# Rows of three expert pairs fetched from DRAM and transposed in place of one-hot products

## The chip, the cores and the metric

The kernel runs on one core of a Trainium2 chip, and the metric is the device time of one execution in microseconds (us). About 0.5% (5.5 us) is what a timing of this kernel can tell from no change.

## What is computed

A two-layer trunk on 512 tokens of width 1024. Layer 0 mixes with attention and a state-space scan, layer 1 with a chunked mLSTM; behind each mixer stands a layer norm, a mixture of experts with 16 experts of hidden width 256, of which two are chosen for each token, and another layer norm. The change concerns only how the experts get their tokens:

```python
combine = jnp.einsum('tk,tke->te', weights, jax.nn.one_hot(expert_id, N_EXPERTS))
hid = jax.nn.silu(jnp.einsum('td,edf->tef', t, w_gate)) * jnp.einsum('td,edf->tef', t, w_up)
hid = hid * combine[:, :, None]
out = jnp.einsum('tef,efd->td', hid, w_down)
```

## The kernel before

Nearly every matrix product runs with both operands split in two float32r parts, high and low, and three matmuls for the four part products (`mm3`, lines 265 to 272: high by high, high by low, low by high). A high part is made by a cast on ScalarE (ACT, line 217) and a low part by a subtraction on VectorE (DVE) or GpSimd (POOL), line 218.

The router (`route`) works on four blocks of 128 tokens. Each token gets a slot in each of its two experts; `cm` holds for each token and expert the slot number (from 1) or 0, and two indirect DMAs a block, issued by POOL (line 970), scatter the token's 16 combine weights into the DRAM table `cd`, one row for each slot. When all four blocks are routed, the table is read back into SBUF as `cb` (the tile `s5bc`, line 1143, on SP's DMA queue), and column 17e of it scales the output of expert e. An expert takes up to 128 tokens; a branch (`overflow`, lines 1231 to 1292) would deal with more and is not taken here.

In `experts` the 16 experts follow each other, two of them a pair. Expert e needs its tokens transposed (`xs`, eight blocks of 128 features by 128 slots), a gate and up product (`gate_up`: 24 matmuls of 512 columns into the PSUM tile `pj`), a gating step with two small transposes (`hidden`), and a down product (12 matmuls of 512 columns into `mm`), whose result is scaled on ACT (line 1186) and written to DRAM (`yd`). The transposed tokens of a pair come from `dispatch`: eight one-hot matrices (DVE, line 1056, 128 by 128 each) say which token sits in which slot, and 64 matmuls of 256 columns (line 1075, tile `tp`: 8 feature blocks by 4 token blocks by the two parts) multiply the tokens by them. While pair p is computed, pair p+1 is prepared, one half in each expert's turn. Pair 0 is prepared in the router (`dispatch_first`, `dispatch_rest`), pairs 1 to 7 in `experts`.

The weights come in pieces of 1 MB (128 by 2048 float32) on SP's queue, three an expert: two for gate and up, one for down. Raw pieces go in turn into one buffer `raw` and two buffers `ca`; a buffer is free for the next load when both parts are made. Of the two `ca` buffers one always holds the down pieces, whose low part POOL makes (experts 1 to 13). The fourth piece goes into a buffer of its own, `raw2`. The parts lie in four pairs of slots (`wh`/`wl` and `x8`), so a piece can be split when PE is done with the piece four before it.

Every engine runs its instructions in order. The order is made by a scheduler from the program and its dependences, so an edit can also move instructions that it does not touch. POOL's queue holds the scatters, the low parts of the down pieces and, behind the last of them, the eight gathers of the outputs (`gather`, line 1206).

Of the kernel before, what the change touches and what calls it, by code (L numbers as in the profile page):

```python
# [9 lines left out]
F32 = mybir.dt.float32  # L10
F32R = mybir.dt.float32r
BF16 = mybir.dt.bfloat16
I32 = mybir.dt.int32
# [13 lines left out]
JOIN = "tp", "pj", "sm", "mm"  # L27
JOIN_PE = 2, 3
NLAST = 2


def _f(x):
# [20 lines left out]
class Trunk:  # L53
# [40 lines left out]
    def consts(self):  # L94
# [70 lines left out]
        self.yd = self.dr.tile([2561, 1024], F32, name="yd")  # L165
        self.yo = [self.dr.tile([6145, 512], F32, name=f"yo{i}") for i in range(2)]

        self.cd = self.dr.tile([8192, 16], F32, name="cd")
        self.co = self.dr.tile([8192, 16], F32, name="co")
        self.xr = [None] * 4  # L170

# [25 lines left out]
    def zero_rows(self, i):  # L197

        nc = self.nc
        z = self.t("t", [128, 512])  # L200
        nc.gpsimd.memset(z, 0.0)
        if i == 0:
            for h in range(2):
                nc.sync.dma_start(self.yd[2560:2561, h * 512:(h + 1) * 512], z[0:1])
                nc.sync.dma_start(self.yo[h][0:1, :], z[0:1])
                nc.sync.dma_start(self.cd[0:2048, :].rearrange("(p a) b -> p (a b)", p=128), z[:, 0:256])
# [680 lines left out]
    def route(self, tb, layer, gb, lT, mu, rs, first):  # L887
# [7 lines left out]
        for _ in first:  # L895
# [29 lines left out]
        selb = self.sm("rsb", [128, 16], BF16, bufs=8)  # L925
        V.tensor_copy(selb, sel.rearrange("p a b -> p (a b)"))
        spl = self.split(xs[0], xs[1], x)
        if tb == 0:
            self.selbs, self.cm, self.xs, self.ses = [], [], [], []
            self.rows = self.sm("rrow", [128, 4, 2])  # L930
            self.pos = self.sm("rpos", [128, 4, 2], I32)
# [9 lines left out]
        cm = self.sm("rcm", [128, 16], bufs=8)  # L941
# [16 lines left out]

        gs = self.sm("rgsum", [128, 1])
        V.tensor_reduce(gs, ex[:, 0, :], axis=AX.X, op=ALU.add)  # L960
        se = self.sm("rse", [128, 16], bufs=5)
        self.ses.append(se)
        es = self.sm("res", [128, 1])
        V.scalar_tensor_tensor(se, ex[:, 1:5, :].rearrange("p a b -> p (a b)"), 1.0, s16,
# [3 lines left out]
        V.tensor_scalar(se, se, es, 1.0 / ALPHA, op0=ALU.mult, op1=ALU.mult)  # L968
        def scatter(r, deps=False):
            ins = nc.gpsimd.indirect_dma_start(  # L970
                out=self.cd[:, :], out_offset=bass.IndirectOffsetOnAxis(ap=pos[:, r:r + 1], axis=0),
                in_=se, in_offset=None)
            if deps:
                self.after(ins, [self.last_pow])

# [139 lines left out]
    def pair_parts(self, p, out, back=None):  # L1115

        cms = [[c[:, e:e + 1] for c in self.cm] for e in (2 * p, 2 * p + 1)]
        for q, tp in self.dispatch(cms, 2, back) if p else self.dispatch_rest():
            if p % 2:
                hl = [self.t("s2", [128, 2, 256], F32R) for _ in range(2)]  # L1120
            else:
                if q % 2 == 0:
                    full = [self.t("xr", [128, 4, 256], F32R) for _ in range(2)]
                hl = [f[:, (q % 2) * 2:(q % 2) * 2 + 2, :] for f in full]
            self.banked.append(self.split(hl[0], hl[1], tp))
            for k in range(2):
                out.append((hl[0][:, k, :], hl[1][:, k, :]))
            yield

    def experts(self, layer):  # L1130
        nc = self.nc
        yd = self.yd[0:2048, :].rearrange("(p e) d -> e p d", e=16)
        base = self.piece_i
        x = []
        self.banked = []
        self.onehots(self.oh3, 3)
        self.overflow(layer, base)
        for _ in self.pair_parts(0, x):
            pass
        self.flush()  # L1140
        self.sources()
        cb = self.sm("s5bc", [128, 256], bufs=1)
        nc.sync.dma_start(cb, self.cd[0:2048, :].rearrange("(p e) c -> p (e c)", e=16))
        back, last, gus, xs, used = [], [], {}, {0: x}, iter(range(48))
        prep = None

        def gate_up(e):
            es = slice((e % 2) * 128, (e % 2 + 1) * 128)
            gus[e] = gu = self.p("pj", [128, 512])
            for q in range(2):  # L1150
                w = self.moe_piece(base, 3 * e + q, next(used))
                for k in range(4):
                    xk = xs[e // 2][q * 4 + k]
                    self.mm3(gu, xk, w, q == 0 and k == 0, q == 1 and k == 3, np.s_[:, es], np.s_[:, k, :])

        for e in range(16):
            if e % 2 == 0 and e < 14:
                xs[e // 2 + 1] = []
                prep = self.pair_parts(e // 2 + 1, xs[e // 2 + 1], back if e == 12 else None)
# [12 lines left out]
            w = self.moe_piece(base, 3 * e + 2, next(used))  # L1172
            c = cb[:, 17 * e:17 * e + 1]
# [452 lines left out]
```

## Time and profile before

| | us |
|---|---|
| median of 3 runs (1103.36 to 1108.22) | 1107.16 |
| the profiled execution | 1107.95 |
| its span, first to last instruction | 1106.1 |
| PE busy in the span | 1031.3 (93%) |
| DVE, ACT, POOL busy | 785.8, 543.1, 353.2 |

PE (TensorE) is busy in nearly all of the span. The granted clock of TensorE is 0.974 of full speed over the whole run. The two expert stages lie at about 329 to 515 us and 878 to 1062 us; in these the DMA engines are busiest too. An entry of the profile counts a matmul from its start to its modelled end, and neighbours overlap, so the distance from start to start tells what one costs.

### The profile page before, as it was taken

The page shows a single profiled execution, that of the slowest core. Times are in us where ns is not written, and L with a number is a line of the kernel's source. Part 1 is how long each engine was busy: PE and PEld are TensorE (multiplying, and loading weights), DVE is VectorE, ACT ScalarE, POOL GpSimd, SP SyncE. Part 2 cuts the span into 40 slices and gives each one's busy share as a digit, 9 for nine tenths or more (in the row PEclk, how much of TensorE's full clock was granted, in tenths as well). Part 3 has the DMA queues.
Part 4 walks back from the last instruction along what each step waited for, and adds up shares of the span by engine and source line. Part 5 has one row for each costly group of instructions (what it writes and reads, how often), then busy time and mean ns, then how long its engine had stood idle before and what let it go on. Part 6 is the DMA issues. An engine that isn't in the chain of part 4 may idle for free. (4 is left out here: it accounts for less than half of the span.)

```text
span 1106.1 us, 14794 instructions
## 1 busy us (share of the span) xinstructions
PE 1031.3 (93%) x5570; PEld 833.6 (75%) x5570; DVE 785.8 (71%) x1422; ACT 543.1 (49%) x754; POOL 353.2 (32%) x218
## 2 busy tenths in 40 slices
PE   7879999999979999999899999999999899999995
PEld 5677767767768877778587989898877788878773
DVE  7885889787786766656555766667888866757665
ACT  5223554572256666666354444444512467756652
POOL 4077455001123442322433333331002333333332
PEclk9988999999989999999899999999999899999998
DMA  7312223333147786767732221222322477868775
GB/s 232 110 55 89 97 65 94 121 126 146 36 164 257 282 299 257 267 241 260 192 120 96 69 82 63 74 77 77 114 77 86 152 267 270 290 254 287 275 265 147
DMA packets 48347, 180.62 MB, mean 163 GB/s; under 512 B 17588, under 2 KB 18516, under 8 KB 32264
## 3 DMA queue, kind: packets, MB, share of 16 engines
q1 hardware_dynamic: 41240, 156.11, 40.7%
q0 software_dynamic: 2992, 8.77, 3.3%
q10 hardware_dynamic: 4032, 14.68, 3.2%
q8 instruction: 46, 0.75, 0.3%
q14 instruction: 37, 0.30, 0.1%
HBM read 155.94 MB, written 22.42 MB: 161 GB/s over the span
## 5 line engine op out<-in xcount | busy, mean ns | idle before, releaser
L270 PE MATMUL pj<-x,wh 128*128 128x512 f32 x288 | 117.8, 409 | 6.1 <-ACT x L217 5.7
L217 ACT CAST wh<-raw 128x2048 fp32r<-128x2048 f32 (+1 forms) x49 | 88.2, 1800 | 57.3 <-DMA raw<-in_w 41.3
L271 PE MATMUL pj<-x,wh 128*128 128x512 f32 x288 | 116.3, 404 | 0.0
L272 PE MATMUL pj<-x,wl 128*128 128x512 f32 x288 | 115.7, 402 | 0.0
L1075 PEld LDWEIGHTS tp<-t,a 128*128 128x128 f32 x896 | 110.8, 191 | 3.0 <-ACT pt L1067 0.6
L1075 PE MATMUL tp<-t,a 128*128 128x256 f32 x896 | 111.8, 283 | 0.0
L218 POOL TENSOR_TENSOR wl<-raw,wh 128x2048 fp32r<-128x2048 f32 x15 | 69.3, 4620 | 132.4 <-ACT wh L217 132.4
L218 POOL TENSOR_TENSOR x<-ca,x 128x2048 fp32r<-128x2048 f32 x14 | 64.7, 4622 | 134.5 <-ACT x L217 101.2
L218 DVE TENSOR_TENSOR wl<-raw,wh 128x2048 fp32r<-128x2048 f32 (+1 forms) x34 | 73.2, 2153 | 45.4 <-ACT wh L217 45.1
L218 DVE TENSOR_TENSOR wl<-ca,wh 128x2048 fp32r<-128x2048 f32 x18 | 41.2, 2291 | 71.4 <-ACT wh L217 65.5
L218 POOL TENSOR_TENSOR wl<-ca,wh 128x2048 fp32r<-128x2048 f32 x12 | 57.4, 4784 | 98.4 <-ACT wh L217 90.5
L1186 ACT ACTIVATE a<-mm,s5bc 128x512 f32<-128x512 f32 x56 | 38.3, 687 | 70.4 <-PE mm L272 70.4
L217 ACT CAST x<-ca 128x2048 fp32r<-128x2048 f32 (+1 forms) x40 | 66.1, 1653 | 13.2 <-DMA ca<-in_w 4.8
L270 PEld LDWEIGHTS pj<-x,wh 128*128 128x128 f32 x288 | 56.0, 194 | 18.2 <-ACT x L217 6.7
L271 PEld LDWEIGHTS pj<-x,wh 128*128 128x128 f32 x288 | 55.6, 193 | 12.0 <-DVE x L218 1.3
L272 PEld LDWEIGHTS pj<-x,wl 128*128 128x128 f32 x288 | 55.5, 193 | 11.0
L217 ACT CAST wh<-ca 128x2048 fp32r<-128x2048 f32 x30 | 57.1, 1903 | 10.2 <-DMA ca<-in_w 10.0
L290 POOL TENSOR_TENSOR lnrs<-lnve,nhalf 128x1 f32<-128x1 f32 x16 | 14.7, 924 | 138.3 <-DVE lnve L301 103.5
L1056 DVE TENSOR_SCALAR t<-iota,rcm 128x128 fp32r<-128x128 f32 x112 | 56.8, 551 | 0.4
L270 PE MATMUL pj<-wh,x 128*128 128x256 f32 x192 | 55.9, 291 | 0.0
L271 PE MATMUL pj<-wl,x 128*128 128x256 f32 x192 | 55.3, 288 | 0.0
L272 PE MATMUL pj<-wh,x 128*128 128x256 f32 x192 | 55.0, 286 | 0.0
(513 smaller groups left out, 2824.0 us busy)
## 6 DMA issues: line engine op xcount, KB each, us to landing
raw<-in_w SPq DMA_DIRECT2D x63, 1024.0 KB, 5.3
ca<-in_w SPq DMA_DIRECT2D x62, 1024.0 KB, 5.1
yd<-a ACTq DMA_DIRECT2D x28, 512.0 KB, 6.1
a<-in_w SPq DMA_DIRECT2D x6, 512.0 KB, 6.6
yd<-t SPq DMA_DIRECT2D x6, 512.0 KB, 3.1
ca<-in_xT SPq DMA_DIRECT2D x8, 256.0 KB, 5.8
a<-in_ln SPq DMA_DIRECT2D x4, 512.0 KB, 5.0
xr<-in_x SPq DMA_DIRECT2D x4, 512.0 KB, 6.2
```

The costliest lines, as they stand in the source:

```text
L217: a = nc.scalar.copy(h, src)
L218: b = (eng or nc.vector).tensor_sub(l, src, h.bitcast(F32))
L270: nc.tensor.matmul(ps, lhsT=aH[ai], rhs=bH[bi], start=first, stop=False)
L271: nc.tensor.matmul(ps, lhsT=aH[ai], rhs=bL[bi], start=False, stop=False)
L272: nc.tensor.matmul(ps, lhsT=aL[ai], rhs=bH[bi], start=False, stop=last)
L290: self.last_pow = self.nc.gpsimd.tensor_tensor(rs, ve, self.nhalf, op=ALU.pow)
L1056: ins = nc.vector.tensor_scalar(oh[:, j, m * 128:(m + 1) * 128], self.iota1, c[2 * i + j], None, op0=ALU.is_equal)
L1075: nc.tensor.matmul(tp[:, k, :], lhsT=self.xs[tb][i][:, cs], rhs=ohs[tb], start=tb + i == 0, stop=tb + i == 4)
L1186: nc.scalar.activation(yo[:, ns], ps, AF.Copy, scale=c)
```

## The change

Pairs 1, 3 and 5 (`FETCHED`) get their tokens in another way; pairs 0, 2, 4, 6 and 7 keep the one-hot products.

- Each layer's normalized tokens are written to DRAM as `x1d`, 512 KB for each block of 128 tokens, on ACT's DMA queue, right behind the split of the block.
- The rows of `cd` get a 17th column with the token's number; a free slot keeps 1024, a number past the last token. There is one `cd` for each layer, both filled at the start. ACT writes the number (a 128 by 1 instruction a block).
- When `cb` has landed, DVE turns the numbers into integers (`rtok`; for the first pair free slots are set to 511, for the others a fetch leaves rows past 511 out). POOL then fetches the rows of the pair's two experts from `x1d` with two indirect DMAs of 128 rows by 4 KB into `raw2`, the buffer that the fourth weight piece has left.
- For each expert PE transposes eight 128 by 128 blocks (`tok_T`), and ACT and DVE split the result in two parts as before.
- The fetch of pair 3 is issued behind expert 1's preparation, the one of pair 5 behind expert 5's.
- The loads of the first four weight pieces stand ahead of the fetch in the program.

```diff
+FETCHED = 1, 3, 5
-        self.cd = self.dr.tile([8192, 16], F32, name="cd")
+        self.cd = [self.dr.tile([8192, 17], F32, name=f"cd{i}") for i in range(2)]
+        self.x1d = [self.dr.tile([512, 1024], F32, name=f"x1d{i}") for i in range(2)]
...
         spl = self.split(xs[0], xs[1], x)
+        nc.scalar.dma_start(self.x1d[layer][tb * 128:(tb + 1) * 128, :], x)
...
-        se = self.sm("rse", [128, 16], bufs=5)
+        row = self.sm("rse", [128, 17], bufs=5)
+        nc.scalar.activation(row[:, 16:17], self.rover[:, tb:tb + 1], AF.Copy, bias=-2048.0)
+        se = row[:, 0:16]
...
+    def row_parts(self, p, xg, out):
+        for e in range(2):
+            for q, tp in self.tok_T(xg[:, e, :]):
+                hl = [self.t("s2", [128, 4, 128], F32R) for _ in range(2)]
+                self.split(hl[0], hl[1], tp)
+                for k in range(4):
+                    out[2 * p + e].append((hl[0][:, k, :], hl[1][:, k, :]))
+                yield
...
+        tok = self.sm("rtok", [128, 16], I32, bufs=1)
+        tv = cb.rearrange("p (e c) -> p e c", c=17)[:, :, 16]
+        V.tensor_scalar(tok[:, 0:4], tv[:, 0:4], 511.0, None, op0=ALU.min)
+        V.tensor_copy(tok[:, 4:16], tv[:, 4:16])
+        ahead = [self.moe_piece(base, j, j) for j in range(4)]
+        xg = self.t("raw2", [128, 2, 1024])
+        def fetch(p):
+            for e in range(2):
+                nc.gpsimd.indirect_dma_start(
+                    out=xg[:, e, :], out_offset=None, in_=self.x1d[layer][:, :],
+                    in_offset=bass.IndirectOffsetOnAxis(ap=tok[:, 2 * p + e:2 * p + e + 1], axis=0),
+                    bounds_check=511, oob_is_err=p == FETCHED[0])
+        fetch(FETCHED[0])
...
+                if p in FETCHED:
+                    prep = self.row_parts(p, xg, xs)
+                else:
+                    prep = self.pair_parts(p, xs, back if e == 12 else None)
...
+            if e % 2 and (e + 1) // 2 in FETCHED[:-1]:
+                fetch((e + 1) // 2 + 2)
```

How the order moves is shown for the start of the second layer's expert stage. On PE, before, the last matmul of expert 0's gate and up product (`pj_9180`) is followed by pair 1's first 32 products, then the gating transposes (`sm`), then expert 1's gate and up product (`pj_9304`):

```order
L272 MATMUL pj_9180<-x_1838_9200,xr_9150 128x512
L1075 MATMUL tp_9227<-t_9217,a_8063 128x256
L1075 MATMUL tp_9227<-t_9217,a_8064 128x256
L1075 MATMUL tp_9227<-t_9217,a_8205 128x256
L1075 MATMUL tp_9227<-t_9217,a_8206 128x256
L1075 MATMUL tp_9227<-t_9222,a_8346 128x256
L1075 MATMUL tp_9227<-t_9222,a_8347 128x256
L1075 MATMUL tp_9227<-t_9222,a_8548 128x256
L1075 MATMUL tp_9227<-t_9222,a_8549 128x256
```

These are the first 8 of the 32. On PE, now, at the same place, with `raw_1843` the fetched rows and `pj_9156` expert 1's gate and up product:

```order
L280 MATMUL pj_9084<-x_1835_9060,xr_9020 128x512
L278 MATMUL pj_9156<-x_1841_9072,xr_9005 128x512
L279 MATMUL pj_9156<-x_1842_9073,xr_9005 128x512
L280 MATMUL pj_9156<-x_1841_9072,xr_9006 128x512
L278 MATMUL pj_9156<-x_1841_9072,xr_9005 128x512
L1054 MATMUL tp_9109<-ident,raw_1843_9077 128x128 x4
L1054 MATMUL tp_9118<-ident,raw_1843_9077 128x128 x4
L279 MATMUL pj_9156<-x_1842_9073,xr_9005 128x512
L280 MATMUL pj_9156<-x_1841_9072,xr_9006 128x512
```

Four matmuls of expert 1 now stand ahead of the pair's first eight transposes, the other 20 behind them. On ACT, now, at that place (`t_9127` is expert 0's gating, `x_1873` and `x_1883` are high parts of weight pieces):

```order
L225 CAST wh_9170<-raw_9169 128x2048
L225 CAST x_1873_9223<-ca_9222 128x2048
L225 CAST s_1846_9114<-tp_9109 128x512
L1041 ACTIVATE t_9127<-pj_9084 128x256
L225 CAST s_1849_9123<-tp_9118 128x512
L225 CAST pt_9134<-sm_9131 128x256
L225 CAST x_1883_9266<-raw_9265 128x2048
```

The cast of the transposed rows (`s_1846<-tp`) stands ahead of expert 0's gating, which stood ahead of the pair's casts before. On POOL, now, the scatters (`cd`), the fetches (`raw_1843<-x1d`) and the low parts of the down pieces of experts 1 to 6:

```order
L981 DMA cd_138<-rse_8462,rpos_7955 8192x17 x2
L1178 DMA raw_1843_9077<-x1d_140,rtok_9050 128x1024 x2
L226 TENSOR_TENSOR x_1874_9224<-ca_9222,x_1873_9223 128x2048
L1178 DMA raw_1843_9077<-x1d_140,rtok_9050 128x1024 x2
L226 TENSOR_TENSOR wl_9346<-ca_9344,wh_9345 128x2048
L226 TENSOR_TENSOR x_1918_9458<-ca_9456,x_1917_9457 128x2048
L226 TENSOR_TENSOR wl_9548<-ca_9546,wh_9547 128x2048
L1178 DMA raw_1843_9077<-x1d_140,rtok_9050 128x1024
L226 TENSOR_TENSOR x_1964_9644<-ca_9642,x_1963_9643 128x2048
L1178 DMA raw_1843_9077<-x1d_140,rtok_9050 128x1024
L226 TENSOR_TENSOR wl_9766<-ca_9764,wh_9765 128x2048
```

Before, the low parts followed the scatters without anything between; now pair 1's fetches stand ahead of the first, pair 3's ahead of the second, and pair 5's ahead of the fifth and the sixth.

## Rows read from the trace of the kernel before

**Rows 1.** Profile page, busy time: engine, us (share of span), instructions.

```profile
PE 1031.3 (93%) x5570; PEld 833.6 (75%) x5570; DVE 785.8 (71%) x1422; ACT 543.1 (49%) x754; POOL 353.2 (32%) x218
```

**Rows 2.** Windows: us; PE, PEld, DVE, ACT, POOL busy (count); PEclk; DMA share; GB/s.

```profile
328.80:515.00 186.20, 176.27 (x970) 149.03 (x969) 120.94 (x146) 115.40 (x124) 61.74 (x14) 0.98 0.74 266
878.50:1062.00 183.50, 175.79 (x983) 149.10 (x982) 120.44 (x146) 116.57 (x125) 60.83 (x13) 1.00 0.76 271
```

**Rows 3.** Timeline of PE, pair 1's first half: start, us, instruction.

```profile
878.49 3.99 PE L1075 MATMUL tp<-t,a 128*128 128x256 f32 x32
```

**Rows 4.** Timeline of PE, eight transposes of another stage.

```profile
551.44 1.03 PE L1043 MATMUL tp<-ident,xr 128*128 128x128 f32 x8
```

**Rows 5.** Chain of waits in the second expert stage: start, us, what.

```profile
946.79 4.64 POOL wl L218
951.45 5.72 DMA ca<-in_w
957.25 1.91 ACT x L217
959.28 4.64 POOL x L218
...
981.22 0.23 PE pj L270
```

**Rows 6.** Timeline of POOL, low parts of down pieces, both layers.

```profile
330.95 4.68 POOL L218 TENSOR_TENSOR x<-ca,x 128x2048 fp32r<-128x2048 f32 x1 [8.57 <-ACT x L217]
...
385.63 4.62 POOL L218 TENSOR_TENSOR x<-ca,x 128x2048 fp32r<-128x2048 f32 x1 [7.47 <-ACT x L217]
...
398.86 4.62 POOL L218 TENSOR_TENSOR wl<-ca,wh 128x2048 fp32r<-128x2048 f32 x1 [8.61 <-ACT wh L217]
...
497.55 4.61 POOL L218 TENSOR_TENSOR x<-ca,x 128x2048 fp32r<-128x2048 f32 x1 [11.47 <-ACT x L217]
...
880.46 4.71 POOL L218 TENSOR_TENSOR x<-ca,x 128x2048 fp32r<-128x2048 f32 x1 [9.52 <-ACT x L217]
...
1041.51 4.62 POOL L218 TENSOR_TENSOR x<-ca,x 128x2048 fp32r<-128x2048 f32 x1 [10.54 <-ACT x L217]
```

**Rows 7.** Timeline of SP's queue, then landing times of the tile s5bc.

```profile
874.67 0.33 SPq L1143 DMA_DIRECT2D s5bc<-cd  x1
...
DMA to landing us min/median/max: 2.0/2.4/2.8
```

**Rows 8.** Timeline of DVE at that place: start, us, instruction.

```profile
873.35 0.16 DVE L1000 TENSOR_SCALAR rsr<-rsr 128x8 f32<-128x8 int32 x1
...
876.20 2.29 DVE L218 TENSOR_TENSOR x<-raw,x 128x2048 fp32r<-128x2048 f32 x1
```

**Rows 9.** The output gathers' line: ns min/median/max, first and last start; landing.

```profile
L1206 POOL DMA_INDIRECT xr<-yd,rsrc x16: 941/1541/2656, 523.4 to 1080.2; - x16
...
DMA to landing us min/median/max: 5.7/7.3/10.0
```

**Rows 10.** PE idle at the stage's start, then granted clock (columns of rows 2).

```profile
869.40 0.98 PE L1111 MATMUL mm<-pt,a 128*128 128x256 f32 x3 [3.31 <-PEq L1236]
...
867.00:870.00 3.00, 0.60 (x3) 0.63 (x4) 2.85 (x3) 0.00 (x0) 1.25 (x2) 0.55 0.02 5
870.00:874.10 4.10, 4.10 (x16) 3.62 (x16) 3.30 (x11) 1.75 (x3) 0.94 (x1) 0.50 0.75 262
```

**Rows 11.** One-hots on DVE, and PE behind them, pair 5 of layer 1.

```profile
974.24 3.55 DVE L1056 TENSOR_SCALAR t<-iota,rcm 128x128 fp32r<-128x128 f32 x5
...
978.18 0.50 PE L272 MATMUL mm<-x,pt 128*128 128x512 f32 x1 [2.17 <-DVE pt L218]
```

**Rows 12.** PE at the same place of layer 0, and its clock.

```profile
429.89 0.50 PE L272 MATMUL mm<-x,pt 128*128 128x512 f32 x1 [2.07 <-DVE pt L218]
...
430.20:433.80 3.60, 3.60 (x10) 2.81 (x9) 0.02 (x1) 2.20 (x2) 0.00 (x0) 0.53 0.66 271
```

**Rows 13.** Profile page, DMA issues: KB each, median us to landing.

```profile
yd<-a ACTq DMA_DIRECT2D x28, 512.0 KB, 6.1
```

More of the change, by code (lines that the diff above doesn't have):

```diff
@@ L205, in zero_rows @@
                 nc.sync.dma_start(self.yo[h][0:1, :], z[0:1])
-                nc.sync.dma_start(self.cd[0:2048, :].rearrange("(p a) b -> p (a b)", p=128), z[:, 0:256])
+            zc = self.t("t", [128, 16, 17])
+            nc.gpsimd.memset(zc, 0.0)
+            nc.gpsimd.memset(zc[:, :, 16], 1024.0)
+            for cd in self.cd:
+                nc.sync.dma_start(cd[0:2048, :].rearrange("(p a) b -> p (a b)", p=128), zc.rearrange("p a b -> p (a b)"))
         own = self.yd[2048:2560, :].rearrange("(p r) (h d) -> p (r h) d", p=128, h=2)
@@ L924, in route @@
                                op0=ALU.is_lt, op1=ALU.mult)
[L925 removed]
+        selb = self.sm("rsb", [128, 16], BF16, bufs=6)
         V.tensor_copy(selb, sel.rearrange("p a b -> p (a b)"))
         spl = self.split(xs[0], xs[1], x)
+        nc.scalar.dma_start(self.x1d[layer][tb * 128:(tb + 1) * 128, :], x)
         if tb == 0:
@@ L940, in route @@
         s16 = sel.rearrange("p a b -> p (a b)")
-        cm = self.sm("rcm", [128, 16], bufs=8)
+        cm = self.sm("rcm", [128, 16], bufs=6)
         cmi = V.scalar_tensor_tensor(cm, cnt, 1.0, s16, op0=ALU.add, op1=ALU.mult)
@@ L970, in scatter @@
             ins = nc.gpsimd.indirect_dma_start(
-                out=self.cd[:, :], out_offset=bass.IndirectOffsetOnAxis(ap=pos[:, r:r + 1], axis=0),
-                in_=se, in_offset=None)
+                out=self.cd[layer][:, :], out_offset=bass.IndirectOffsetOnAxis(ap=pos[:, r:r + 1], axis=0),
+                in_=row, in_offset=None)
             if deps:
@@ L1126, in pair_parts @@
             for k in range(2):
-                out.append((hl[0][:, k, :], hl[1][:, k, :]))
+                for e in range(2):
+                    es = np.s_[:, k, e * 128:(e + 1) * 128]
+                    out[2 * p + e].append((hl[0][es], hl[1][es]))
             yield
+    def row_parts(self, p, xg, out):
[6 more added lines that the diff above has]
+                yield
     def experts(self, layer):
@@ L1133, in experts @@
         base = self.piece_i
-        x = []
+        V = nc.vector
+        xs = {e: [] for e in range(16)}
         self.banked = []
@@ L1137, in experts @@
         self.overflow(layer, base)
-        for _ in self.pair_parts(0, x):
+        for _ in self.pair_parts(0, xs):
             pass
@@ L1141, in experts, with piece @@
         self.sources()
-        cb = self.sm("s5bc", [128, 256], bufs=1)
-        nc.sync.dma_start(cb, self.cd[0:2048, :].rearrange("(p e) c -> p (e c)", e=16))
-        back, last, gus, xs, used = [], [], {}, {0: x}, iter(range(48))
+        cb = self.sm("s5bc", [128, 272], bufs=1)
+        nc.sync.dma_start(cb, self.cd[layer][0:2048, :].rearrange("(p e) c -> p (e c)", e=16))
+        tok = self.sm("rtok", [128, 16], I32, bufs=1)
[5 more added lines that the diff above has]
+        def fetch(p):
+            for e in range(2):
+                nc.gpsimd.indirect_dma_start(
[3 more added lines that the diff above has]
+        fetch(FETCHED[0])
+        back, last, gus, used = [], [], {}, iter(range(48))
         prep = None
+        def piece(i):
+            j = next(used)
+            return ahead[j] if j < 4 else self.moe_piece(base, i, j)
         def gate_up(e):
-            es = slice((e % 2) * 128, (e % 2 + 1) * 128)
             gus[e] = gu = self.p("pj", [128, 512])
             for q in range(2):
-                w = self.moe_piece(base, 3 * e + q, next(used))
+                w = piece(3 * e + q)
                 for k in range(4):
-                    xk = xs[e // 2][q * 4 + k]
-                    self.mm3(gu, xk, w, q == 0 and k == 0, q == 1 and k == 3, np.s_[:, es], np.s_[:, k, :])
+                    self.mm3(gu, xs[e][q * 4 + k], w, q == 0 and k == 0, q == 1 and k == 3, np.s_[:, :], np.s_[:, k, :])
         for e in range(16):
             if e % 2 == 0 and e < 14:
-                xs[e // 2 + 1] = []
-                prep = self.pair_parts(e // 2 + 1, xs[e // 2 + 1], back if e == 12 else None)
+                p = e // 2 + 1
+                if p in FETCHED:
+                    prep = self.row_parts(p, xg, xs)
+                else:
+                    prep = self.pair_parts(p, xs, back if e == 12 else None)
             if e < 15:
@@ L1171, in experts @@
                 self.join(1, None, None)
-            w = self.moe_piece(base, 3 * e + 2, next(used))
-            c = cb[:, 17 * e:17 * e + 1]
+            w = piece(3 * e + 2)
+            c = cb[:, 18 * e:18 * e + 1]
             if e < 16 - NLAST:
```

## Prediction

> **What bounds the kernel now.** I read the busy times first: PE is busy 93% of the span and every other engine far less [rows 1]. A share over the whole span says nothing of one stage, so the windows came next, one for each expert stage. There PE is busy 176.3 of 186.2 us and 175.8 of 183.5 us, DVE and ACT near 120, POOL near 61, the DMA engines at three quarters, and the granted clock is 0.98 and 1.00 [rows 2]. The reader is to see that PE has 9.9 and 7.7 us of idle time to lose, and that what is taken off PE can become time. Then the chain of waits, to see what stands close behind PE: it runs long stretches through the buffer of the down pieces (POOL's low part 4.64 us, the next load 5.72, ACT's cast 1.91, POOL again), a lap of 959.28 − 946.79 = 12.5 us for each expert [rows 5]. That is about what PE needs for an expert, (1041.51 − 880.46) / 12 = 13.4 us with all its stalls [rows 6]. So PE is first, and the supply of weights a close second. Last I read the timelines around the start of the second stage, where the new fetch has to fit in.
>
> **Taken off PE.** 32 products, half a pair, take 3.99 us, 0.12 us from start to start [rows 3]; a pair has 64, 7.7 us. Eight transposes of this size take 1.03 us with the tail of the last, 0.11 from start to start [rows 4]; a fetched pair needs 16, 1.8 us. A pair saves 5.9 us, and with three pairs in each of two layers PE loses 6 x 5.9 = 35.4 us of work.
>
> **The first fetch, a new wait.** The old pair 1 needed one-hots only and PE went on without a gap at 878.49. Now the chain is: last scatter, load of the table, two DVE instructions, fetch, transposes. The table's load is issued at 874.67, when the scatters have landed, and lands in 2.0 to 2.8 us, median 2.4 [rows 7]: 877.1. The two DVE instructions have 4 and 12 columns; one of 8 columns takes 0.16 [rows 8], so 0.4 with their starts: 877.5. The buffer must be free too: its last reader, the low part of the fourth weight piece, ran from 876.20 to 878.5 behind eight one-hots [rows 8], and without these it is over before 877. The nearest operation to the fetch is the gather of outputs, 128 rows of 4 KB by POOL: 0.9 to 2.7 us of POOL, and landing 5.7 to 10.0 us after issue, median 7.3 in a queue of eight [rows 9]. The fetch meets an empty queue and no accumulation, so I take 6.0, near the low end; the bounds are 2.0, the least landing of the little table [rows 7], and 10.0. Rows are there at 883.5. PE, at 0.23 a matmul [rows 5], has its four matmuls of expert 1 done at 879.4 and then waits 4.1 us (0.1 to 8.1). The other 20 matmuls, which would cover it, are queued behind the transposes. Expert 0's gating on ACT is queued there as well, behind the cast of the rows; PE needs it only after 12 more matmuls, so this costs nothing more.
>
> The wait has a second price. PE idled 3.31 us before 869.40, and the clock was granted at 0.55 and 0.50, the 1.2 GHz level, until 874.1 [rows 10]: half of 4.7 us of work, 2.3 us. I take the same behind this wait (0 to 3.4). Together 6.4 us in each layer, 12.8 in all: pair 1 gives back what it saves.
>
> The Trainium skill, in "DMA: Bandwidth & Descriptors", section "Anatomy of one DMA — SWDGE (gpsimd) path", puts a DMA issued by GpSimd at about 2.0 us plus its bytes at 436 GB/s, which would be 3.2 us for one fetch of 512 KB, an estimate. By that the wait is 1.3 us and the sum about 6 us lower; the gathers here never came below 5.7 [rows 9], so the row is kept.
>
> **The other fetches.** Pair 3's two are issued when PE has transposed pair 1's rows, near 894 us for the second, and are used two laps of 12.5 and a gate and up product later, some 30 us; pair 5's likewise. Wait: none. But they stand in POOL's queue. Behind the second waits the low part of expert 2's down piece: two fetches at some 1.5 us [rows 9] move it about 3 us, while PE has 24 matmuls and half a pair of products (9.4 us) ahead of the product that needs it. Cost zero, and 3 us a layer if that lead is gone.
>
> **Stalls that go.** The one-hots of pair 5 ran beside POOL's low part, five in 3.55 us, and PE waited 2.17 us for the DVE instruction queued behind them [rows 11]; in layer 0 it was 2.07 us, and the clock then fell to the lower level for 3.6 us [rows 12], 1.7 us more. Pair 5 has no one-hots now: 5.9 us, between 0 and 5.9, since the same can happen to pairs 2, 4, 6 and 7. I take it whole and set the next step against it.
>
> **What is late next.** An expert of a fetched pair takes PE about 3 us less, 9.6 us of its 12.5, while the down buffer's lap stays at 12.5. In the meantime PE lives on the pieces already split, at most four. Over twelve laps the chain took 161.1 and 166.6 us [rows 6]; at 12.5 it could do 150, so it has room for 11 and 16.6 us, 27.6 in both. That just holds the gain that I forecast. I charge 2 us a layer for loads that come late, 4 in all (0 to 17, the rival below).
>
> **Edits at no cost.** The four writes of `x1d` are 512 KB each; such a write lands in 6.1 us [rows 13], the last is issued near 859 and read at 877, and its issue stands behind a cast. The 17th column adds a small ACT instruction a block and 64 bytes a partition to the table's load; the 48 one-hots a layer that DVE loses add nothing beyond the stalls above.
>
> **Sum.** The profiled execution took 1107.95 us, 0.8 above the median of the runs. −35.4 + 12.8 − 5.9 + 4 = −24.5, so 1083.5 us.
>
> **Rivals.** *The weights set the pace.* If the down buffer's lap lengthens as loads and fetches crowd, to the 398.86 − 385.63 = 13.2 us that it also shows [rows 6], twelve laps take 158.8 us and leave 2.3 and 7.8 us to gain: 1098. For it: the lap is that close, and POOL's fetches stand in its queue. Against: four split pieces and three raw ones, over two experts' worth, can be run down first.
> *Everything hides.* The first rows come within 1 us of being needed, the clock holds, and no load is late: −35.4 − 5.9, plus 1, about 1068. For it: the fast end of the landing. Against: no gather here was as fast.
> *Slower: each pair waits like the first.* If the fetches of pairs 3 and 5 reach PE late by the same 4.1 us and drop the clock, six pairs cost 6 x 6.4 = 38.4 against 35.4, and no stall goes: 1111. It decides from a wait plus clock loss of 5.9 us a pair. For it: one buffer serves all fetches, so a fetch can't be issued before the pair two ahead is transposed, and POOL holds it behind its low parts. Against: 30 us of cover where I count 8 as needed.
>
> **How the numbers follow.** Forecast 0.60, with its own range 1074 to 1092: a landing at 2.0 or 10.0 in place of 6.0 moves the sum by 8 either way. Weights set the pace 0.20, everything hides 0.12, slower 0.05, and 0.03 for some loss that leaves the time where it is. From 1069 to 1100 leaves out half of the fast rival, the slower ones and the upper tail of the second, some 2 in 10. Faster by over 0.5% (5.5 us, what a measurement here can tell): the forecast, the fast rival and nearly all of the second, 0.88; within it 0.06; slower 0.06.
>
> **What would show it.** In the profile after: 512 products on line 1086 in place of the 896 on 1075, and 96 transposes more at 0.11 us apart; at both stages' starts PE idle 3 to 5 us until the fetched rows (`raw<-x1d`) land and then about 4.7 us at the lower clock; no wait for `raw<-x1d` at pairs 3 and 5; POOL's first and last low part 138 to 150 us apart in each layer, less than before. The forecast is wrong if PE stands idle in the fetched pairs behind ACT's casts and loads (the second rival), or if the first wait is under 1 us or over 8.

## The result, and the profile after

The changed kernel takes 1091.3 us (median of 4 runs, 1087.91 to 1092.03); the kernel before took 1106.74 beside it. The ratio is 0.9851 with a 95% interval of 0.9824 to 0.9878: 16.5 us faster (13.5 to 19.5). The forecast was 1083.5, so two thirds of the forecast gain came. The profiled execution took 1091.48 us, its span is 1089.8.

The profile page's busy times after (engine, us, share of the span, instructions) answer to [rows 1]:

```profile
PE 1000.1 (92%) x5282; PEld 801.1 (74%) x5282; DVE 770.8 (71%) x1378; ACT 543.2 (50%) x762; POOL 370.6 (34%) x232
```

The reader is to subtract. The span fell from 1106.1 to 1089.8, by 16.3. PE's busy time fell by 31.2, and its idle time (span less busy) rose from 74.8 to 89.7, by 14.9. The work went as forecast; half of it came back as waiting.

Where the waiting lies, the expert stages show. A mark that both kernels have is the write of an expert's output on ACT's queue, 14 in a layer (the last two experts' outputs stay on the chip). From the first to the last, 13 experts pass. The windows between these marks, before and then after (columns as in [rows 2]):

```profile
337.70:519.80 182.10, 172.17 (x936) 145.05 (x935) 117.72 (x141) 113.51 (x121) 57.06 (x13) 0.98 0.75 267
887.20:1063.80 176.60, 168.89 (x936) 142.86 (x935) 116.91 (x141) 113.41 (x121) 56.12 (x12) 1.00 0.77 276
```

```profile
339.30:506.80 167.50, 155.18 (x800) 129.12 (x799) 111.24 (x126) 113.53 (x122) 61.94 (x16) 0.97 0.80 291
878.50:1047.40 168.90, 155.40 (x799) 128.51 (x798) 110.64 (x126) 112.88 (x121) 62.57 (x15) 0.97 0.80 290
```

The 13 experts are 14.6 us shorter in layer 0 and 7.7 in layer 1, together more than the span. Some 3 us in each are no gain: at the first mark PE now has all 24 matmuls of expert 1's gate and up product behind it, where it had 8, and at the last mark 3 matmuls more of the next one, at 0.23 us each. Both layers now take nearly the same time, 167.5 and 168.9, where before they took 182.1 and 176.6. PE's idle time in them went from 9.9 and 7.7 to 12.3 and 13.5. The clock fell from 0.98 and 1.00 to 0.97.

The first fetch in layer 1: the timeline of POOL with the two fetches of pair 1, then PE's first transposes (line 1054), then the landing times of all twelve fetches:

```profile
865.15 1.07 POOL L1178 DMA_INDIRECT raw<-x1d,rtok  x1 [7.24 <-DVE rsr L1020]
866.52 2.34 POOL L1178 DMA_INDIRECT raw<-x1d,rtok  x1 [0.31 <-issue]
868.89 4.60 POOL L226 TENSOR_TENSOR x<-ca,x 128x2048 fp32r<-128x2048 f32 x1
...
869.53 1.09 PE L1054 MATMUL tp<-ident,raw 128*128 128x128 f32 x8 [3.01 <-DMA raw<-x1d,rtok]
...
DMA to landing us min/median/max: 4.3/7.3/9.9
```

The rows came 4.3 us after the issue and PE stood for 3.01 us (2.93 in layer 0). The clock behind this wait, in the window of the next 5 us, was full (1.00 in layer 0, too):

```profile
869.50:874.50 5.00, 4.97 (x27) 4.04 (x27) 2.37 (x5) 1.73 (x4) 4.84 (x2) 1.00 0.76 294
```

By lines, PE's new transposes and the products left over (busy us, mean ns, idle before):

```profile
L1054 PE MATMUL tp<-ident,raw 128*128 128x128 f32 x96 | 13.5, 273 | 5.9 <-DMA raw<-x1d,rtok 5.9
L1086 PE MATMUL tp<-t,a 128*128 128x256 f32 x512 | 67.0, 286 | 1.2 <-DVE s L226 1.2
```

All the waiting for fetched rows is 5.9 us, and the two first fetches are 2.93 + 3.01 = 5.9 of it: pairs 3 and 5 never waited for rows.

What PE waits for in layer 1 now (total, times, longest):

```profile
PE pj L279 <- DVE wl L226: 5.2, 3, 2.3
PE pj L279 <- DVE x L226: 3.1, 3, 1.4
PE tp L1054 <- DMA raw<-x1d,rtok: 3.0, 1, 3.0
PE sm L1046 <- DVE t L1043: 2.8, 3, 1.6
```

The stall of pair 5 [rows 11] is gone. In its place stand the low parts of gate and up pieces on DVE (line 226, the first two rows), for none of which PE waited as long as 0.4 us in this layer before, and the gating on DVE (the last row). The place of [rows 11], an expert later, by timelines of ACT, POOL, DVE and PE in this order:

```profile
971.39 1.91 ACT L225 CAST x<-ca 128x2048 fp32r<-128x2048 f32 x1 [3.42 <-DMA ca<-in_w]
...
973.43 4.60 POOL L226 TENSOR_TENSOR x<-ca,x 128x2048 fp32r<-128x2048 f32 x1 [8.56 <-ACT x L225]
...
973.94 4.18 DVE L1067 TENSOR_SCALAR t<-iota,rcm 128x128 fp32r<-128x128 f32 x1
...
979.68 2.28 DVE L226 TENSOR_TENSOR wl<-ca,wh 128x2048 fp32r<-128x2048 f32 x1
...
979.03 0.44 PE L1046 MATMUL sm<-ident,t 128*128 128x128 f32 x2 [1.60 <-DVE t L1043]
...
982.01 0.79 PE L279 MATMUL pj<-wl,s 128*128 128x512 f32 x1 [2.31 <-DVE wl L226]
```

ACT, and everything queued behind its cast, stood 3.42 us for a load. Then a one-hot for pair 6 took 4.18 us on DVE while POOL ran its low part. The gating queued behind it came late, and PE waited 1.60 us; the next piece's low part came only at 979.68, and PE waited 2.31 us for it. Layer 0 has the same one-hot of 4.18 us (at 435.49) and the same two waits. So 3.9 of the 12.3 and 13.5 us that PE is idle in the 13 experts stand behind one stretched one-hot. Behind the second wait the clock fell to the 1.2 GHz level:

```profile
982.00:987.40 5.40, 5.39 (x13) 4.22 (x14) 4.08 (x6) 1.90 (x1) 1.44 (x1) 0.50 1.02 408
```

POOL's low parts of the down pieces, the first at 868.89 (above) and the last of layer 1, and both of layer 0, against [rows 6]:

```profile
329.52 4.60 POOL L226 TENSOR_TENSOR x<-ca,x 128x2048 fp32r<-128x2048 f32 x1
...
486.37 4.63 POOL L226 TENSOR_TENSOR x<-ca,x 128x2048 fp32r<-128x2048 f32 x1 [7.97 <-ACT x L225]
...
1025.12 4.61 POOL L226 TENSOR_TENSOR x<-ca,x 128x2048 fp32r<-128x2048 f32 x1 [8.02 <-ACT x L225]
```

Twelve laps, from the first low part to the last, take 156.9 and 156.2 us, 13.0 on average, where 166.6 and 161.1 stood before. Single laps take from 11.5 to 15.2 us.

### The profile page after: what moved, and what is told of

It reads as the page before. It is cut to its first block, busy times and chain, and to the rows that moved or that the text cites. A ratio compares the mean times of both kernels' runs of the same rounds, so it can differ in the third digit from the quotient of the medians.

```text
span 1089.8 us, 14241 instructions
## 1 busy us (share of the span) xinstructions
PE 1000.1 (92%) x5282; PEld 801.1 (74%) x5282; DVE 770.8 (71%) x1378; ACT 543.2 (50%) x762; POOL 370.6 (34%) x232
## 4 chain that ended last, share of the span: by engine, by line
PE 47%; DMA 16%; DVE 15%; ACT 7%; POOL 5%; issue 3%; POOLq 0%; ACTq 0%; DVEq 0%
PE pj L279 8%; PE pj L278 8%; PE pj L280 8%; DMA ca<-in_w 5%; DMA cd<-rse,rpos 5%; DMA raw<-in_w 3%; PE tp L1086 3%; DVE wl L226 3%; POOL wl L226 3%; ACT x L225 2%; PE mm L278 2%; PE mm L280 2%; PE mm L279 2%; ACT wh L225 2%; DMA xr<-yd,rsrc 2%
## 5 line engine op out<-in xcount | busy, mean ns | idle before, releaser
L278 PE MATMUL pj<-x,wh 128*128 128x512 f32 x288 | 116.3, 404 | 5.7 <-ACT x L225 5.4
L279 PE MATMUL pj<-x,wh 128*128 128x512 f32 x288 | 114.9, 400 | 0.0
L226 POOL TENSOR_TENSOR x<-ca,x 128x2048 fp32r<-128x2048 f32 x14 | 67.0, 4789 | 93.8 <-ACT x L225 93.8
L226 DVE TENSOR_TENSOR wl<-raw,wh 128x2048 fp32r<-128x2048 f32 (+1 forms) x34 | 72.7, 2139 | 17.6 <-ACT wh L225 17.6
L226 DVE TENSOR_TENSOR x<-ca,x 128x2048 fp32r<-128x2048 f32 (+1 forms) x26 | 47.3, 1819 | 42.4 <-ACT x L225 42.3
L1086 PEld LDWEIGHTS tp<-t,a 128*128 128x128 f32 x512 | 66.0, 194 | 3.9 <-DVE s L226 1.6
L1086 PE MATMUL tp<-t,a 128*128 128x256 f32 x512 | 67.0, 286 | 1.2 <-DVE s L226 1.2
```

The costliest lines, as they stand in the source:

```text
L226: b = (eng or nc.vector).tensor_sub(l, src, h.bitcast(F32))
L278: nc.tensor.matmul(ps, lhsT=aH[ai], rhs=bH[bi], start=first, stop=False)
L279: nc.tensor.matmul(ps, lhsT=aH[ai], rhs=bL[bi], start=False, stop=False)
L1086: nc.tensor.matmul(tp[:, k, :], lhsT=self.xs[tb][i][:, cs], rhs=ohs[tb], start=tb + i == 0, stop=tb + i == 4)
```

## Experiments

Two theories were put against each other. *Supply*: the chain of a weight piece (load into a raw buffer, cast on ACT, low part on DVE or POOL, next load) can't follow a PE that needs less time for an expert. In the later runs it is told by the time that one raw buffer takes to go round, and is called the lap theory. *One-hots*: the remaining one-hots, stretched beside POOL's low parts, hold up DVE's low parts. Beside them stood the question of what the first wait costs. All ratios are to the kernel before on the same chip; 0.01 is 11 us.

**Pairs 3 and 5 alone.**

```diff
-FETCHED = 1, 3, 5
+FETCHED = 3, 5
...
-                    bounds_check=511, oob_is_err=p == FETCHED[0])
+                    bounds_check=511, oob_is_err=False)
```

> Pairs 3 and 5 fetched as in the changed kernel, pair 1 by one-hots as before (the fetch of pair 3 then is the first). The prediction priced pair 1's fetch at about nothing (-5.9 us of PE work, +6.4 of wait and lower clock in a layer): then this kernel is within 1 us of the changed one, 1090 to 1092. The changed kernel's trace shows only 3.0 us of wait and no lower clock behind it, so pair 1 should be worth 2.9 us a layer: 1097. Supply theory (the weight pieces' loads, casts and low parts can't follow a PE that needs 9.6 us for an expert, so what PE is spared early is waited for later): 1091 to 1093, with fewer stalls behind low parts of weights later in the stage.

Measured: 1098.78, ratio 0.9941 (0.9914 to 0.9969), 6.5 us. That is near the 1097 which the changed kernel's own wait gives, and not in the supply theory's 1091 to 1093.

**Pair 1 alone.**

```diff
-FETCHED = 1, 3, 5
+FETCHED = 1,
```

> Only pair 1 fetched, pairs 3 and 5 by one-hots as before. By the prediction's price for pair 1: 1107, no change from before. By the changed kernel's trace (3.0 us of wait against 5.9 of work): 1101. Supply theory: pairs 3 and 5 bring little over this, so 1093 to 1097. One-hot theory (one-hots on DVE, stretched beside POOL's low parts, hold up the weights' low parts on DVE): pair 5's one-hots are back and with them its stall of 2.2 us, 1101 to 1104.

Measured: 1094.5, ratio 0.9900 (0.9867 to 0.9933), 11 us, in the supply theory's range. Pair 1, which the prediction held to give back what it saves, gives no less than the other two pairs together, though PE waits 3.8 and 3.4 us for its rows here too. The two parts add up to the whole (6.5 + 11 = 17.5 against 16.5). Pairs 3 and 5 save 23.6 us of PE work and bring 6.5. The 13 experts took 170.0 and 171.4 us with pairs 3 and 5, and 169.4 and 171.2 with pair 1 alone, against 167.5 and 168.9 with all three. PE's idle time in these windows is 12.0 and 13.0 us with pairs 3 and 5, and 7.3 and 9.0 with pair 1 alone, about as much as before: the added waiting comes with pairs 3 and 5. The profile of pair 1's kernel has its limit: the profiled execution was the slowest of six, 5 us above their median.

With pairs 3 and 5 alone, PE also stood 8.07 us for a one-hot of pair 4, which was queued on DVE behind the low part of a late weight piece (PE, then DVE, then ACT's cast of that piece):

```profile
939.99 0.55 PE L1086 MATMUL tp<-t,a 128*128 128x256 f32 x1 [8.07 <-DVE t L1067]
...
935.63 2.29 DVE L226 TENSOR_TENSOR x<-raw,x 128x2048 fp32r<-128x2048 f32 x1 [7.45 <-ACT x L225]
...
933.71 1.90 ACT L225 CAST x<-raw 128x2048 fp32r<-128x2048 f32 x1 [3.54 <-DMA raw<-in_w]
```

The name behind the arrow is a one-hot, but what came late is the load: this is how supply looks through an engine that works in order.

**Pairs 2, 4 and 6 in place of 1, 3 and 5.** The rows' parts go into `xr`, and free slots are set to 511 up to pair 2.

```diff
-FETCHED = 1, 3, 5
+FETCHED = 2, 4, 6
...
-        V.tensor_scalar(tok[:, 0:4], tv[:, 0:4], 511.0, None, op0=ALU.min)
+        V.tensor_scalar(tok[:, 0:6], tv[:, 0:6], 511.0, None, op0=ALU.min)
...
```

> The same number of fetched pairs as in the changed kernel, but pairs 2, 4 and 6, so that PE has pair 1's products to do while the first rows come (the rows' low parts stand in the larger buffer of the even pairs). If the first wait costs its 3.0 us in each layer and the rest is as in the changed kernel: 1085. By the prediction's price of it (6.4 a layer): 1078. Supply theory: the 3 us come back as stalls behind weight pieces, 1089 to 1092, and PE shows no idle time behind fetched rows.

Measured: 1100.4, ratio 0.9950 (0.9924 to 0.9977). A miss of every expected time: no idle time stands behind fetched rows, and it is still about 11 us slower than the changed kernel. Against the kernel before, PE's busy time fell by 29.0 us and its idle time rose by 21.5, mostly in waits for DVE. Why this choice of pairs fits the supply worse was not settled.

**Pairs 1 to 6.** A half of the buffer is fetched again behind each expert, and the parts of an even pair go into `xr`:

```diff
-FETCHED = 1, 3, 5
+FETCHED = 1, 2, 3, 4, 5, 6
...
-            if e % 2 and (e + 1) // 2 in FETCHED[:-1]:
-                fetch((e + 1) // 2 + 2)
+            if e < 10:
+                fetch(e // 2 + 2, (e % 2,))
```

> All of pairs 1 to 6 fetched, one expert's rows at a time (a half of the buffer is fetched again as soon as PE has transposed it). Another 35.4 us of PE work goes, and 48 one-hots a layer with it. Supply theory: the lap of an expert is 12.5 to 13 us whatever PE does, twelve laps 150 to 156 us, so nearly nothing is gained: 1085 to 1092, with PE idle 20 us more in each stage behind casts and low parts of weights. One-hot theory: without the one-hots DVE's low parts come on time and POOL's run at 4.2 us: 1060 to 1072.

Measured: 1100.77, ratio 0.9956 (0.9926 to 0.9985): above the supply theory's 1085 to 1092, and far from the one-hot theory's 1060 to 1072. The PE work fell by another 22.6 us of busy time (977.5) and the time rose. The 13 experts of layer 1, in the window between the output writes (layer 0 has 165.4):

```profile
886.40:1051.50 165.10, 138.05 (x639) 109.18 (x639) 103.23 (x101) 110.92 (x120) 74.06 (x21) 0.96 0.82 299
```

PE is idle 27 of 165 us, where the changed kernel has 13.5 of 168.9; for its 17 us less of work the stage is 4 us shorter. Its whole span is 7 us longer all the same (1096.8), and 5.8 of these stand ahead of the second stage, where PE waited longer before the same product (the changed kernel, then this one; PEq is PE's sequencer, and "issue" means that the profile shows nothing waited for):

```profile
856.24 0.98 PE L1122 MATMUL mm<-pt,a 128*128 128x256 f32 x3 [3.39 <-PEq L1283]
...
865.02 0.80 PE L1122 MATMUL mm<-pt,a 128*128 128x256 f32 x3 [9.22 <-issue]
```

The profiled execution of the same pairs with halves (below) has such a wait of 8.4 us, the other kernels none above 3.9. What makes it, and whether every execution has it, is open; so up to half of the rise may have nothing to do with the weights.

With most one-hots gone the waits for low parts are more, so the one-hot theory can't be the main one. The raw buffer of the gate and up pieces beside the down pieces' shows what sets the pace (timelines of POOL, DVE, ACT and PE, in order of time):

```profile
944.54 4.63 POOL L226 TENSOR_TENSOR wl<-ca,wh 128x2048 fp32r<-128x2048 f32 x1 [3.87 <-ACT wh L225]
...
948.47 2.86 DVE L226 TENSOR_TENSOR x<-ca,x 128x2048 fp32r<-128x2048 f32 x1 [4.15 <-ACT x L225]
...
956.93 4.60 POOL L226 TENSOR_TENSOR x<-ca,x 128x2048 fp32r<-128x2048 f32 x1 [4.72 <-ACT x L225]
...
958.48 1.90 ACT L225 CAST wh<-ca 128x2048 fp32r<-128x2048 f32 x1
...
960.41 3.27 DVE L226 TENSOR_TENSOR wl<-ca,wh 128x2048 fp32r<-128x2048 f32 x1 [4.57 <-PE tp L1054]
...
963.73 0.50 PE L279 MATMUL pj<-wl,xr 128*128 128x512 f32 x1 [2.47 <-DVE wl L226]
```

The buffer is free at 948.47 + 2.86 = 951.33; the next piece is loaded into it, its cast ends at 960.38, its low part at 963.68: a lap of 12.35 us, and PE takes up the piece 0.05 us later. (The arrow at 960.41 names PE; ACT's cast of this very piece ended 0.03 us before.) The down pieces' lap is 956.93 − 944.54 = 12.39. So two of the three raw buffers go round in 12 to 13 us, and they are tied: both low parts on DVE were started while POOL's ran (still 4.6 us each), took more than the usual 2.29 us, and ended 2.15 us behind POOL's end (949.17 and 961.53), as if they had only begun there. The Trainium skill has this rule in "SBUF — State Buffer", section "Who interferes with whom": a DVE operation with two inputs in SBUF, or in a two-port mode, and a POOL operation that reads SBUF exclude each other, and the one that comes second waits for the other's end. The trace agrees to 0.15 us. The one-hot at 973.94 in the changed kernel, ended 0.09 us behind POOL's, agrees too if it ran in such a mode, which no row here tells.

**Half the bytes in layer 1.** The pieces behind the fourth of layer 1 leave out their second half; the cast reads the first half twice, so casts and low parts are as long as before and the output is another one:

```diff
...
-            nc.sync.dma_start(raw, src)
+            nc.sync.dma_start(raw[:, :1024], src[:, :1024])
+            rv = raw[:, None, :1024].to_broadcast([128, 2, 1024])
...
```

> The changed kernel, but in layer 1 each weight piece after the first four loads only its first half (512 KB in place of 1 MB) and the cast reads that half twice, so the output is another one; casts and low parts take as long as before, layer 0 is left as it is. Lap theory (PE waits for the lap of a raw buffer: load 6.4 us, cast 1.9, low part 2.3 to 4.6, with one buffer for the pieces that are the first of an expert and one for the last): loads land 2 to 3 us earlier, the lap comes under PE's need, twelve of POOL's laps in layer 1 fall from 156 to about 145 us, layer 1's stage is 8 to 14 us shorter than layer 0's, and the time 1077 to 1083. One-hot theory (DVE's one-hots, stretched beside POOL, are what delays the low parts): the load is not what is late, 1089 to 1092, and the stalls of layer 1 stand where they stood.

Measured: 1084.95, ratio 0.9790 (0.9758 to 0.9823), between the two theories and nearer to the lap theory's 1077 to 1083. Landing of the `ca` loads in layer 1, in the changed kernel and here:

```profile
DMA to landing us min/median/max: 4.7/5.5/7.6
```

```profile
DMA to landing us min/median/max: 3.2/3.8/5.3
```

Layer 1's 13 experts fell from 168.9 to 161.4 us, layer 0's stayed (167.0): loads 1.7 us shorter give 7.5 us over 13 experts. So the load is part of what sets the pace. The gain is less than the lap theory's: POOL's twelve laps took 150.0 us and not 145, and two waits of 1.8 us for a low part remain in layer 1.

**All low parts on DVE.**

```diff
-                               eng=self.nc.gpsimd if i % 3 == 2 and 2 < i < 42 else None,
+                               eng=None,
```

> The changed kernel with all low parts of the weights on DVE (2.3 us each) and none on POOL (4.6 us beside DVE's work). DVE gets 13 x 2.3 = 30 us more in each layer, of some 75 us that it has free there. If the down pieces' buffer with POOL's 4.6 us sets the pace (the prediction's rival): its lap falls by 2.3 us and the time by 10 us or more, 1075 to 1082. If the buffer of the first pieces (low part on DVE) sets it: that lap loses only what POOL's work beside it costs DVE (low parts of 2.9 to 3.3 us back to 2.3) and gains a queue, so 1085 to 1092.

Measured: 1086.85, ratio 0.9794 (0.9762 to 0.9826); the 13 experts took 161.4 and 164.4 us, with the first output write later than in the changed kernel (345.0 and 880.6 against 339.3 and 878.5). This is the second of the expected cases. The one-hots of layer 1 (min/median/max ns), in the changed kernel and here:

```profile
L1067 DVE TENSOR_SCALAR t<-iota,rcm x32: 269/275/4207, 879.5 to 1017.7; 128x128 fp32r<-128x128 f32 x32
```

```profile
L1067 DVE TENSOR_SCALAR t<-iota,rcm x32: 274/279/287, 872.1 to 1009.7; 128x128 fp32r<-128x128 f32 x32
```

So the one-hot theory has a true part, and it holds for DVE's low parts as well: beside POOL's low parts single one-hots take up to 4.2 us, without them none does. What that is worth apart from the shorter lap of the down pieces was not separated: the two waits behind a stretched one-hot in each layer of the changed kernel, 7.8 us in all, are more than the whole gain of 6 us.

**Weight pieces in halves.** A piece behind the fourth keeps its raw buffer, but loads, casts and subtracts it in two halves:

```diff
...
+        for c in range(2):
+            nc.sync.dma_start(raw[:, c * 1024:(c + 1) * 1024], src[:, c * 1024:(c + 1) * 1024])
+            cs = np.s_[:, c * a // 2:(c + 1) * a // 2, :]
+            self.split(h[cs], l[cs], raw[:, c * 1024:(c + 1) * 1024].rearrange("p (a b) -> p a b", a=a // 2), eng=eng)
...
```

> The changed kernel with the weight pieces after the first four loaded, cast and subtracted in two halves of 512 KB, each half of the raw buffer loaded again as soon as its own low part is done; the same bytes and the same arithmetic. Lap theory: a half's lap is a load of some 4 to 5 us, a cast of 1.0 and a low part of 1.2 to 2.3, 3 us and more under the whole piece's 12.4, so the stalls behind low parts in the fetched pairs go and the time is 1075 to 1083. If the DMA engines' rate is the limit (share 0.78 of the stage), a half lands as late as a whole did and the time stays at 1088 to 1093. One-hot theory: no gain, or a loss by the fixed cost of twice as many instructions, 1091 to 1097.

Measured: 1091.99, ratio 0.9840 (0.9810 to 0.9870): no gain. The 13 experts are 2.8 and 3.4 us shorter, the stage's start longer (first output write at 342.4 and 880.9 against 339.3 and 878.5). A half landed after 5.4 us (median of the `ca` loads in layer 1), where a whole took 5.5. By themselves halves give nothing with three pairs fetched; the lap theory's 1075 to 1083 was wrong here. What came is the expected case of halves that land as late as wholes did. That the rate of the DMA engines is no fixed limit at this height, the last kernels show: 290 GB/s in layer 1's 13 experts of the changed kernel, 334 in the best one below.

**Pairs 1 to 6 and halves**, the two edits above together.

> Pairs 1 to 6 all fetched, an expert's rows at a time, and the weight pieces in halves as in the kernel just before it. With whole pieces PE lost 35.4 us more of work than in the changed kernel and the time rose by some 10 us. Lap theory: with the shorter lap that work becomes time: 1055 to 1070. If the loads' rate or the order on DVE and ACT sets the pace whatever the buffers: 1085 to 1100.

Measured: 1087.51, ratio 0.9806 (0.9779 to 0.9834), about 16 us under the same pairs with whole pieces. The time lies in the second of the expected ranges, 1085 to 1100, though the gain on whole pieces is clear.

**Pair 1's transposes behind expert 1's product.**

```diff
-            for _ in range(2):
+            for _ in range(0 if e == 0 else 4 if e == 1 else 2):
```

> The changed kernel with pair 1's sixteen transposes behind all 24 matmuls of expert 1's gate and up product, 20 of which stood behind them: at 0.23 us these cover 4.6 us, more than the 2.9 and 3.0 us that PE waits for the fetched rows. If the first wait costs its length: no idle time behind the fetched rows and 6 us less, 1084 to 1086. By the prediction's price of it (6.4 us a layer): 1078 to 1080. Supply theory (time saved at the stage's start is waited for at the weight pieces later): the wait goes and the time stays within 2 us, 1089 to 1093.

Measured: 1095.31, ratio 0.9904 (0.9868 to 0.9940); none of the expectations, rather slower than the changed kernel. PE no longer waits for rows, and stands 5 us (6.3 in layer 0) a little later, PE and then DVE:

```profile
879.41 0.47 PE L1046 MATMUL sm<-ident,t 128*128 128x128 f32 x2 [5.01 <-DVE t L1043]
...
876.21 2.29 DVE L226 TENSOR_TENSOR x<-raw,x 128x2048 fp32r<-128x2048 f32 x1 [6.96 <-ACT x L225]
```

The gating on DVE is queued behind a low part whose load is late (ACT's cast waited 3.04 us for it). A wait taken away at the stage's start comes back a few us later at the weights.

**Pairs 1 to 6, all low parts on DVE**, then **the same with halves**, then **pairs 1, 3 and 5 with both**, all by the edits shown:

> Pairs 1 to 6 all fetched, whole weight pieces, and all low parts on DVE. With POOL's low parts this set of pairs took 10 us more than the changed kernel, with halves 5 us less. Lap theory: the down pieces' buffer falls from 12.4 to some 10 us, the buffer of the first pieces stays near 11.5 to 12.4 (load 6.4, cast 1.9, low part 2.3 and what it stands behind): 1080 to 1090. If the one buffer with POOL's 4.6 us was the only bound: 1060 to 1070, near what PE's work alone asks.

> Pairs 1 to 6 all fetched, weight pieces in halves, all low parts on DVE: both cures of the lap together. Lap theory: a half needs a load of 5.3 us, a cast of 1.05 and a low part of 1.22; PE then has 35 us less work than in the changed kernel and waits less for it: 1065 to 1080. If the loads' rate (3 MB for each expert, landings of halves no earlier than those of wholes) sets the pace: 1083 to 1090, no better than with either cure alone.

> The changed kernel (pairs 1, 3 and 5 fetched) with both cures: weight pieces in halves, all low parts on DVE. With all six pairs fetched both together gave 1062. If the prediction's step of loads that come late is the one that was mis-sized, the change's own gain comes out here: PE's 31 us less work, the old stalls gone, 3 us of wait in each layer: 1072 to 1080. If the two cures pay only where all pairs are fetched (nothing is late here that they would bring forward): 1085 to 1092, as with either cure alone.

Measured: 1084.16, ratio 0.9793 (0.9748 to 0.9838); 1061.82, ratio 0.9595 (0.9556 to 0.9633); 1081.98, ratio 0.9745 (0.9719 to 0.9772). The first lies in the lap theory's range, the second below its 1065 to 1080, and the third 2 us above the range in which the change's own gain comes out. The ratios together, the two cures being low parts on DVE and halves:

| pairs fetched | as changed | low parts on DVE | halves | both |
|---|---|---|---|---|
| 1, 3, 5 | 0.9851 | 0.9794 | 0.9840 | 0.9745 |
| 1 to 6 | 0.9956 | 0.9793 | 0.9806 | 0.9595 |

The two kernels of a column differ by six times the 5.9 us of the prediction, 35 us of PE work, 3.2% of the time. As the supply stands, this work is worth less than nothing; with low parts on DVE it is worth 0.0%, with halves 0.3%, and with both 1.5%. So PE's spared work becomes time only as far as the weights keep up, and with both cures still only half of it does. With both cures and pairs 1 to 6, layer 1's 13 experts read (layer 0 has 146.4):

```profile
868.00:1015.50 147.50, 134.29 (x641) 105.94 (x640) 121.02 (x150) 113.00 (x158) 8.97 (x9) 0.99 0.92 334
```

PE does the work of the same pairs with whole pieces (138.05 busy at a lower clock) in 17.6 us less, and the DMA engines, at 0.82 there, are at 0.92 here. This kernel beats both others, by 4.0% (3.7 to 4.4) against the one before. The kernel before with the two cures and no fetch was not run, so how much they give by themselves is open.

## Why the prediction came out 8 us low

- *What bounds the kernel.* PE first and the supply of weights a close second was the right reading; how close was not.
- *Taken off PE.* Right: 512 products, eight transposes in 1.03 to 1.09 us, busy time 31.2 us less. With the clock's share in it the sum held 32.5 (35.4 less 4.6 of lower clock behind the waits, and 1.7 more spared).
- *The first fetch.* Too dear. Landing 4.3 us for 6.0, wait 2.93 and 3.01 for 4.1, and the clock did not fall behind it: 5.9 us in both layers for 12.8, 6.9 too much. The gathers [rows 9] were the wrong neighbour: they land in a queue of eight, this fetch is one of two; that this is the reason was not tested. The Trainium skill's price ("DMA: Bandwidth & Descriptors", section "Anatomy of one DMA — SWDGE (gpsimd) path"), an estimate of 3.2 us worked out from it, was too low by 1.1, the chosen value too high by 1.7. "Pair 1 gives back what it saves" was wrong: alone it gave 11 us.
- *The other fetches.* Right: no wait for rows at pairs 3 and 5, though they landed as late as 9.9 us after issue.
- *Stalls that go.* The named stalls went, but nothing was saved. The prediction had said that the same can happen to pairs 2, 4, 6 and 7, and took the 5.9 us whole; it happened to pair 6 in both layers, where PE waits 1.60 and 2.31 us and loses clock behind them, against 2.17 and 2.07 before.
- *What is late next.* The step that failed. It charged 4 us. Take the first waits out of PE's idle time: the sum then expected −0.2 us (4 charged, 4.2 of old stalls gone), and 14.9 − 5.9 = +9.0 came, 9.2 too little charged. PE's busy time hides more: without a lower clock behind the first waits the sum asked 37.1 us less (35.4 and 1.7), and 31.2 came, 5.9 short, as the clock in the 13 experts fell from 0.98 and 1.00 to 0.97. The lap of 12.5 us was taken from one stretch of the chain [rows 5] and counted as if it held; it became 13.0 on average, so twelve laps took 156 to 157 us and not 150. Why is not settled: the `ca` loads of layer 0's stage landed after 5.7 us (median) for 4.9 before, those of layer 1's after 5.5 for 5.4. That DVE's low parts stand still while POOL's run was not in the sum. And the chain was only one of two: PE's waits show the gate and up pieces, through DVE, while low parts on DVE in place of POOL's won 6 us. That the split pieces which PE was to live on are then soon used up is argued, not traced piece by piece.
- *Luck.* Two errors of the sum partly cancel: 6.9 us of the first fetch that did not come (2.3 of wait, 4.6 of lower clock), and some 15 of late pieces and stalls that did (9.2 and 5.9). The forecast was nearer than its parts.
- *The rivals.* "The weights set the pace" was right that the weights come late, with laps of 13.0 in place of its 13.2; that loads and fetches crowd shows in layer 0's landings alone. The time lies between the forecast and its 1098, by nearly the middle. Its sign, PE idle in the stage behind casts and loads, came as well. "Each pair waits like the first" is refuted by the 5.9 us on line 1054, and "everything hides" by the same 5.9.
- A part of the 16.3 us is not the change's. Far ahead of both stages, in the first mixer, the profiled execution of before ran 6.8 us at half clock and that of after did not (the same window, before and then after):

```profile
95.90:102.70 6.80, 6.80 (x22) 5.64 (x22) 2.32 (x2) 2.97 (x3) 5.40 (x5) 0.50 0.39 133
```

```profile
95.90:102.70 6.80, 6.80 (x37) 5.78 (x37) 3.32 (x2) 2.92 (x3) 5.78 (x4) 1.00 0.41 133
```

After is 2.9 us ahead from there on. Of the kernels above, whose programs are the same up to there, some had this stretch (halves; pairs 1 to 6) and some not, so it does not hang on the change; the medians, not the profiles, carry the comparison.

## What to carry over

Where one engine is busy 95% of a stage, look for the loop that feeds it and time one lap for every buffer of it, not only for the one that the chain of waits happens to show. Here a lap of 12.5 us stood 7% under the 13.4 that the busy engine needed for an expert, and of 35 us of work taken off it 16 became time. The cures of the lap should be tried together with the change: with three pairs fetched one alone gave up to 6 us and both 12, with pairs 1 to 6 fetched each gave 17 to 18 and both 40.

## What was not expected of the hardware

- DVE's 128 by 128 one-hot takes 0.275 us (median) and up to 4.2 beside POOL's low part; DVE's low parts of 2.29 us took up to 3.27 in the rows above. Without low parts on POOL the longest one-hot of layer 1 was 0.287. A small low part of DVE that reads a product of PE (128 by 256, at 973.60) took its usual 0.43 us inside the same operation of POOL that stretched the one-hot.
- A load of half the bytes lands in 3.8 us where the other half is left out (the stage then moves 175 GB/s), and in 5.4 where the other half follows (294 GB/s); a whole takes 5.5 (290). In these runs landing follows what is under way, more than a load's own size.
- A wait's length alone does not tell the clock behind it: full behind the 2.93 and 3.01 us above, at the lower level behind the shorter 2.31 us at 982.01, and at the lower level behind 3.40 us at the first fetch of the kernel with pair 1 alone:

```profile
874.00:877.30 3.30, 3.30 (x10) 2.63 (x9) 1.95 (x4) 1.11 (x3) 2.94 (x1) 0.50 0.93 371
```
